# GpSimd and VectorE jump ahead within a block of instruction memory in a linear-attention kernel

## The chip, the cores and the metric

The kernel runs on one core of a Trainium2 chip. The metric is the device time of one execution in microseconds, as the median of several runs. The core has five engines that run side by side, each with an instruction stream of its own: TensorE (PE), VectorE (DVE), ScalarE (ACT), GpSimd (POOL) and SyncE (SP). They wait for each other on semaphores. Data moves between the chip's main memory (HBM) and on-chip memory (SBUF) on 16 DMA engines, which work through queues that SP, ACT and POOL fill.

## The reference

For each of 8 x 12 heads, Q, K and V are 512 x 64 in 32-bit floats, and a ReLU takes the place of the softmax:

```
Q_feat, K_feat = max(0, Q), max(0, K)
KV    = K_feat^T V            (64 x 64 per head)
K_sum = sum of K_feat over the 512 rows
out   = (Q_feat KV) / (Q_feat . K_sum + 1e-10)
```

There is little arithmetic for the bytes: 37.75 MB are read and 12.58 MB written.

## The kernel before, in words

The 96 heads are worked in 12 tiles of 8 heads. A tile of Q, of K or of V is 128 partitions x 2048 elements, 1 MB in HBM. K and V of tile 0 are loaded as they are, by SP and ScalarE, inside a short part that the tile framework handles (lines 95 to 97). `tc.close()` and `tc.compile()` (lines 99 and 100) end that part: all engines meet there. Everything behind is written by hand, engine by engine, with semaphores.

GpSimd (`PL`) issues all other loads. Line 101 is its first instruction behind the closing: it loads Q of tile 0. It then builds an identity matrix (lines 124 to 126), and issues K, V and Q of tiles 1 to 11 in order (`load`, line 114), the DMA turning 32-bit floats into bf16 on the way. The buffers hold 6 tiles, so from tile 7 on a load waits until VectorE and ScalarE have used the tile that lies there. GpSimd also issues the stores of tiles 0 to 9 (`store`, line 122), SP those of tiles 10 and 11.

VectorE (`VE`) first clears two tiles (lines 289 and 290), casts the identity and makes masks from it (292 to 302). Then it waits for K and V of tile 0 and per tile makes masked, ReLU-ed K (`kf`, line 248) and masked V (`vo`, line 254), copies Q (line 260), computes the denominators and their reciprocals (279 to 287), and multiplies the result out of PSUM by them (line 273), which is what a store waits for.

TensorE runs a loop over the tiles (line 198): it transposes Q, forms K^T V, multiplies Q by it, and transposes back. Line 94, ahead of the tile part, already places TensorE's stream at the start of a block of 256 instructions in the same way that the change uses for two other engines. ScalarE copies out of PSUM and applies the ReLU to Q. Last, SP waits for the final stores and clears the semaphores (lines 323 to 328).

The instructions of an engine lie one behind the other in memory, 64 bytes each, and the engine's sequencer has them fetched by DMA in blocks. In the profile these fetches are the queues of the kind "instruction".

Of the kernel before, what the change touches and what calls it, by code (L numbers as in the profile page):

```python
# [5 lines left out]
def kernel(  # L6
# [25 lines left out]
    PE, PL, VE, AC, SP = nc.tensor, nc.gpsimd, nc.vector, nc.scalar, nc.sync  # L32
# [11 lines left out]
    def sems(*names):  # L44
        new = [nc.alloc_semaphore(n) for n in names]
        handles.extend(new)
        return new
# [40 lines left out]
    def land(name):  # L88
        landed[name], = sems(name)
        return landed[name]  # L90
# [7 lines left out]

    tc.close()
    tc.compile()  # L100
    PL.dma_start(out=q_all[:, RING], in_=Qr[0], single_packet=True).then_inc(land("q0"), 16)
    run_of = {0: 0}

# [253 lines left out]
```

## Time and profile before

| | us |
|---|---|
| median of 3 runs | 124.32 |
| fastest and slowest of them | 124.25, 124.49 |
| the profiled execution, its own time | 124.49 |
| its span, first to last instruction of the kernel | 122.7 |
| VectorE busy / TensorE busy / ScalarE busy | 87.7 / 86.2 / 79.4 |
| GpSimd busy | 27.6 |

The span leaves out what the runtime runs ahead of the kernel's first instruction and behind its last; the own time is 1.79 us longer. In the rows of the page, the line "DMA" gives in tenths how busy the 16 DMA engines are in 40 slices of the span, and the part on queues gives packets, megabytes and the share of the 16 engines' span. In a timeline a row reads: start, duration, engine, line, operation, output and input, and in brackets the idle time before it and what ended it. Beside the views, the trace keeps a record of each DMA packet (queue, start, duration, size) and of each instruction that is not counted as busy (branches, waits); some numbers below come from these records. Times in them are from the start of the span.

### The profile page before, as it was taken

The page shows a single profiled execution, that of the slowest core. Times are in us where ns is not written, and L with a number is a line of the kernel's source. Part 1 is how long each engine was busy: PE and PEld are TensorE (multiplying, and loading weights), DVE is VectorE, ACT ScalarE, POOL GpSimd, SP SyncE. Part 2 cuts the span into 40 slices and gives each one's busy share as a digit, 9 for nine tenths or more (in the row PEclk, how much of TensorE's full clock was granted, in tenths as well). Part 3 has the DMA queues.
Part 4 walks back from the last instruction along what each step waited for, and adds up shares of the span by engine and source line. Part 5 has one row for each costly group of instructions (what it writes and reads, how often), then busy time and mean ns, then how long its engine had stood idle before and what let it go on. Part 6 is the DMA issues. An engine that isn't in the chain of part 4 may idle for free.

```text
span 122.7 us, 3406 instructions
## 1 busy us (share of the span) xinstructions
PE 86.2 (70%) x1480; PEld 73.4 (60%) x1480; DVE 87.7 (71%) x163; ACT 79.4 (65%) x109; POOL 27.6 (23%) x50
## 2 busy tenths in 40 slices
PE   0000099998998989899898998989898199491000
PEld 0000099986896958779595887958687189271000
DVE  1808806499999899999989999899992983761000
ACT  0043062999988888998888989888998196600000
POOL 1899900042140603409201001010010010000000
PEclk9999999999999999999999999999999999999555
DMA  2999999999999999999999999999999999999994
GB/s 64 414 319 214 214 214 214 214 211 214 214 214 211 215 212 215 212 214 214 214 212 214 214 214 214 214 214 350 239 204 286 430 430 427 419 430 430 427 427 190
DMA packets 6915, 32.54 MB, mean 265 GB/s; under 512 B 768, under 2 KB 768, under 8 KB 5120
## 3 DMA queue, kind: packets, MB, share of 16 engines
q0 software_dynamic: 6336, 28.31, 92.9%
q1 hardware_dynamic: 432, 3.15, 6.2%
q10 hardware_dynamic: 144, 1.05, 2.2%
q8 instruction: 1, 0.02, 0.1%
q14 instruction: 2, 0.02, 0.0%
HBM read 37.75 MB, written 12.58 MB: 410 GB/s over the span
## 4 chain that ended last, share of the span: by engine, by line
DMA 39%; PE 28%; DVE 20%; issue 1%; POOL 1%; ACT 1%; DVEq 0%; SPq 0%
DMA q_all<-in_Q_dram 32%; DVE o_sb L273 13%; PE ps_kv L173 12%; DMA o_sb<-in_K_dram 7%; PE ps_o L154 7%; PE ps_q L166 6%; PE ps_o L194 4%; DVE kf L248 3%; DVE vo L254 2%; DVE q_sb L260 1%; ACT ot L234 1%; POOL v_all L114 1%; POOL k_all L114 0%; DVE den L284 0%; PE ps_q L186 0%
## 5 line engine op out<-in xcount | busy, mean ns | idle before, releaser
L273 DVE TENSOR_TENSOR o_sb<-ps_o,rec 128x1024 f32<-128x1024 f32 x24 | 28.3, 1219 | 6.0 <-PE ps_o L154 6.0
L234 ACT COPY ot<-ps_o 128x1024 f32<-128x1024 f32 x24 | 24.2, 1013 | 7.6 <-PE ps_o L194 6.2
L173 PE MATMUL ps_kv<-vo,kf 64*128 64x132 bf16 x768 | 27.9, 227 | 0.0
L220 ACT ACTIVATE qt_sb<-ps_q 128x1024 bf16<-128x1024 bf16 x24 | 23.4, 1030 | 5.7 <-PE ps_q L166 5.7
L154 PE MATMUL ps_o<-ident,ot 128*128 128x128 f32 x208 | 25.7, 277 | 1.1 <-ACT ot L234 1.1
L173 PEld LDWEIGHTS ps_kv<-vo,kf 64*128 64x128 bf16 x768 | 24.2, 98 | 2.9 <-DVE vo L254 0.2
L154 PEld LDWEIGHTS ps_o<-ident,ot 128*128 128x128 f32 x208 | 22.6, 142 | 2.8 <-ACT ot L234 1.4
L166 PE MATMUL ps_q<-ident,q_sb 128*128 128x128 bf16 x192 | 13.6, 227 | 15.1 <-DVE q_sb L260 15.0
L248 DVE TENSOR_SCALAR kf<-k_all,mask_k 128x1024 bf16<-128x1024 bf16 x44 | 18.4, 461 | 5.3 <-PE ps_kv L173 4.0
L194 PE MATMUL ps_o<-qt_sb,kvd 128*128 128x256 bf16 x104 | 15.7, 275 | 9.1 <-DVE o_sb L273 8.6
L166 PEld LDWEIGHTS ps_q<-ident,q_sb 128*128 128x128 bf16 x192 | 11.6, 101 | 17.6 <-DVE q_sb L260 15.0
L225 ACT CAST kvd<-ps_kv 64x260 bf16<-64x260 f32 x48 | 18.0, 375 | 6.2 <-PE ps_kv L173 5.8
L194 PEld LDWEIGHTS ps_o<-qt_sb,kvd 128*128 128x128 bf16 x104 | 8.2, 98 | 14.3 <-DVE o_sb L273 12.5
L254 DVE TENSOR_SCALAR vo<-v_all,mask_v 128x1024 bf16<-128x1024 bf16 x33 | 14.9, 481 | 0.5 <-DMA v_all<-in_V_dram 0.5
L122 POOL DMA_DIRECT2D out_dram<-o_sb x10 | 5.3, 533 | 37.1 <-DVE o_sb L273 37.1
L114 POOL DMA_DIRECT2D k_all<-in_K_dram x11 | 6.6, 596 | 31.3 <-DVE vo L254 31.1
L214 ACT ACTIVATE vo<-v_all,mask_v 128x1024 bf16<-128x1024 bf16 x11 | 12.7, 1155 | 0.3
L260 DVE COPY q_sb<-q_all 128x2048 bf16<-128x2048 bf16 x12 | 8.3, 689 | 2.0 <-DMA q_all<-in_Q_dram 2.0
L114 POOL DMA_DIRECT2D v_all<-in_V_dram x11 | 8.4, 768 | 0.0
L186 PE MATMUL ps_q<-kvd,qt_sb 128*128 128x16 bf16 x208 | 7.5, 180 | 0.0
L186 PEld LDWEIGHTS ps_q<-kvd,qt_sb 128*128 128x128 bf16 x208 | 7.3, 96 | 0.2
L279 DVE SCALAR_TENSOR_TENSOR own<-ps_q,mask_h 128x256 f32<-128x256 f32 x12 | 5.0, 415 | 2.4 <-PE ps_q L186 2.4
(21 smaller groups left out, 28.7 us busy)
## 6 DMA issues: line engine op xcount, KB each, us to landing
out_dram<-o_sb POOLq DMA_DIRECT2D x10, 1024.0 KB, 39.1
q_all<-in_Q_dram POOLq DMA_DIRECT2D x12, 512.0 KB, 35.2
k_all<-in_K_dram POOLq DMA_DIRECT2D x11, 512.0 KB, 31.8
v_all<-in_V_dram POOLq DMA_DIRECT2D x11, 512.0 KB, 33.7
out_dram<-o_sb SPq DMA_DIRECT2D x2, 1024.0 KB, 8.8
o_sb<-in_V_dram ACTq DMA_DIRECT2D x1, 1024.0 KB, 8.4
o_sb<-in_K_dram SPq DMA_DIRECT2D x1, 1024.0 KB, 8.6
```

The lines of the kernel that those rows point to most:

```text
L114: PL.dma_start(out=t[:, to:to + n], in_=X[o:o + n].rearrange("n p f -> p n f"), single_packet=True).then_inc(land(f"{c}{o}"), 16)
L154: t = PE.transpose(ps_o[j][:, P * v:P * v + P], ot[:, 8 * j + v].rearrange("p h c -> p (h c)"), ident32)
L166: t = PE.transpose(dst[:, u], q_sb[:, j * (U // 2) + u], ident)
L173: t = PE.matmul(ps_kv[:, half, 0:2 * (D + 2)].rearrange("p (t d) -> p t d", t=2), kf[g][rows, r].rearrange("p s d -> p (s d)"), vo[g][rows ...
L186: t = PE.matmul(ps_den[:, u], qt_sb[:, u], kvd[:, :, 0:2 * D1:2 * D1 - 1], start=True, stop=True, skip_group_check=True)
L194: t = PE.matmul(ps[:, h], kvd[:, 4 * j + h, 1:2 * D + 1], q[:, :, 4 * j + h, :], start=True, stop=True, skip_group_check=True)
L220: AC.activation(qt_sb[:, j * (U // 2):(j + 1) * (U // 2)], ps_q[j].bitcast(bf16).rearrange("p (u f) -> p u f", u=U // 2), Act.Relu)
L225: t = AC.copy(kvd[64 * c:64 * c + 64, s::2, c * D1:c * D1 + D1].rearrange("p (g t) d -> p g t d", t=2), ps_kv[64 * s:64 * s + 64, :, 0:2 * ...
L234: t = AC.copy(ot[:, :, 4 * j:4 * j + 4], ps_o[j].rearrange("p (h u c) -> p u h c", h=4, u=U))
L248: VE.tensor_scalar(kf[g][:, :, s, :], k_rows(o, g), scalar1=0.0, scalar2=mask_k[:, s:s + 1], op0=Alu.max, op1=Alu.mult)
L254: x = VE.tensor_scalar(vo[g][:, :, t, 2:D + 2], v_rows(o, g), scalar1=mask_v[:, t:t + 1], scalar2=None, op0=Alu.mult)
L273: VE.tensor_tensor(dst[:, rs], ps_o[j].rearrange("p (r d) -> p r d", d=D), rec[o % 2][:, rs].unsqueeze(2).to_broadcast([P, R, D]), op=Alu. ...
```

## The change

Directly behind the closing of the tile part, and ahead of line 101, each of GpSimd and VectorE gets one directive on where its next instruction is to lie. It says: the next instruction goes to the slot that is 112 (for VectorE 120) slots past a multiple of 128 slots, a slot being one instruction of 64 bytes. The slots that are left out are filled with padding when the program is loaded. With `max_nops=0` the engine runs none of the padding: the first of these slots is a branch to the wanted place. No instruction is added beside the branch, none is removed, and the order on every engine stays as it was. Behind the change GpSimd has 16 slots left in its block of 128, and VectorE 8.

```diff
     tc.close()
     tc.compile()
+
+    PL.addr_align(128, offset=112, max_nops=0)
+    VE.addr_align(128, offset=120, max_nops=0)
     PL.dma_start(out=q_all[:, RING], in_=Qr[0], single_packet=True).then_inc(land("q0"), 16)
     run_of = {0: 0}
```

## The prediction

> **What bounds the kernel now.** I read the page's transfer rows first, then the end of the chain of waits, the start of GpSimd's and VectorE's timelines, and last the DMA view in short windows, because what the change moves is instruction memory, and its refills are DMA traffic.
>
> ```profile
> span 122.7 us, 3406 instructions
> ...
> DMA  2999999999999999999999999999999999999994
> ...
> q0 software_dynamic: 6336, 28.31, 92.9%
> ...
> q8 instruction: 1, 0.02, 0.1%
> q14 instruction: 2, 0.02, 0.0%
> HBM read 37.75 MB, written 12.58 MB: 410 GB/s over the span
> ...
> DMA 39%; PE 28%; DVE 20%; issue 1%; POOL 1%; ACT 1%; DVEq 0%; SPq 0%
> ```
>
> The DMA row is 9 in 38 of 40 slices, from 3 us to 120 us: the 16 DMA engines are the bound, not the chain's 39%. The chain runs through TensorE and VectorE because loads wait for buffers to come free, but behind those waits the DMA queue is never empty. The stage view gives it in numbers: DMA share 1.01 to 1.07 in every stage from 3 to 120 us, 427 GB/s from 98 to 120 us. VectorE's last work of weight, the last normalisation, ends at 110.80 us and SP's wait for the last store takes 11.4 us; so compute has some 9 us to spare at the end.
>
> ```profile
> 2.58 0.49 DVE L289 MEMSET kvd<- 128x520 f32 x1 [2.58 <-PEq L100]
> 2.93 0.67 POOL L101 DMA_DIRECT2D q_all<-in_Q_dram  x1 [2.48 <-POOLq L100]
> 3.45 1.76 DVE L290 MEMSET ot<- 128x2048 f32 x1 [0.38 <-issue]
> ...
> 9.65 1.42 DVE L248 TENSOR_SCALAR kf<-o_sb,mask_k 128x1024 bf16<-128x1024 f32 x2 [3.23 <-DMA o_sb<-in_K_dram]
> 9.72 0.81 POOL L114 DMA_DIRECT2D v_all<-in_V_dram  x1
> ```
>
> The timeline of the start, in which the jumps fall. VectorE is idle for 3.23 us ahead of its first real work at 9.65 us. GpSimd issues loads far ahead of what the DMA engines can move: 0.52 us apart, for 1 MB read that takes them 2.46 us.
>
> The DMA view of three windows (42.5 to 43, 48 to 48.5, 123 to 126 us) gives this one line in each:
>
> ```profile
> q14 instruction: 1, 0.01, 4.0%
> ...
> q14 instruction: 1, 0.01, 4.0%
> ...
> q14 instruction: 1, 0.01, 0.7%
> ```
>
> Each is a refill of instruction memory. The packet records put them at 42.55, 48.14 and 124.04 us, each 8,192 bytes and 0.32 us on one DMA engine; 8,192 bytes are 128 instructions of 64 bytes, the block the change counts in. TensorE's, on queue 8, is 16,384 bytes at 1.87 us.
>
> **The change, part by part.**
>
> *The two jumps.* Each engine gets one branch over padding. TensorE's like jump (line 94) has a record of 0.31 us, its loop branches 0.08 to 0.23 us; the floor is nothing, the padding itself being skipped. I take 0.31 us each, the same kind of jump. *VectorE:* its seven set-up instructions move from 2.58 to about 2.9 us and end at 6.75 instead of 6.43; the idle 3.23 us cover that, so 0. ScalarE's table load (6.51 us) waits for the same set-up, but its first activation waits for the V load at 9.29: 0. *GpSimd:* line 101 moves from 2.93 to 3.24 us and all 33 loads behind it on its queue by as much; the identity that VectorE waits for is 0.3 us later, again under the 3.23 us. Would the DMA engines run dry? The first packet of GpSimd's queue is at 6.70 us. Until then K0 and V0, 2.10 MB, fill all 16 engines: 0.17 MB moved by 3 us, then 415 GB/s, so they alone last to 3.0 + 1.93/0.415 = 7.65 us. GpSimd has 0.95 us, the jump takes 0.31: 0 on the path. SP and ScalarE issue K0 and V0 ahead of the change.
>
> *Where blocks are crossed.* From line 101 GpSimd has 49 records, VectorE from line 289 has 177. GpSimd now starts at slot 112: 16 records on (the Q load, the identity's five, ten loads) it crosses at the V load of 9.72 us. It ends at slot 161. VectorE starts at slot 120: seven set-up instructions and the wait for K0, then it crosses at the kf of 9.65 us; the second crossing is 128 records later, the kf at 82.33 us; it ends at slot 297. Which engines cross at 42.55 and 48.14 before, the trace doesn't name. TensorE's jump ends at 1.13 and its refill starts at 1.87, so 0.74 us earlier is 41.8 and 47.4 us; VectorE's copy at 41.72 and GpSimd's load at 41.91 both fit the first. Neither crossing made its engine wait: VectorE's iterations stay 7.26 us apart through both.
>
> *What a refill costs.* The completion writes of each load on the 16 engines are a clock with a period of 2.457 us. At 42.55 one engine falls back by 0.52 us (44.69 expected, 45.21 seen), at 48.14 another by 0.31, and they keep it. So a refill costs 0.31 to 0.52 us on one engine, and the end moves only if that engine is the last, or is made the last. The last store completes on the 16 engines from 120.58 to 121.77, and on one at 122.04 us. After the change there may be up to two more refills in the loaded window (VectorE's second, GpSimd's), so +0 to +0.52 us if the two hit different engines and +1.04 us if both hit the last one; below, a refill gone from the last engine gives at most 122.04 - 121.77 = 0.27 us. With 12 engines finishing at 121.45 or earlier, at least 0.59 us behind, I take 0.
>
> On this the Trainium skill, "Runtime: NRT & Kernel Launch", section "Instruction fetch mechanics", says that crossing a block is one bump of a DMA queue and mostly hidden, with blocks of 16 KiB. The trace agrees for the engine that crosses, not on the size (8,192 bytes but for TensorE), and the 0.31 to 0.52 us on a DMA engine are real. By that rule the term is 0 whatever engine is hit; by the row it is 0 to 1.04 us.
>
> *Sum.* The profiled execution took 124.49 us: span 122.70 and 1.79 around it. 0 + 0 + 0 added to it; it is 0.17 us above the median of 124.32. I forecast 124.35 for the median.
>
> **The rivals.**
>
> *A, the refill of the closing goes (faster).* The fetch at 124.04 ends at 124.37, 0.12 us ahead of the run's own 124.49. If an engine stands there waiting for it, and this engine is GpSimd or VectorE, the jumps take that boundary away: they end at slots 161 and 297, with 95 and 87 slots left in their blocks. The gain is between the transfer's 0.32 us and 0.74 + 0.32 = 1.06 us from crossing to landing: 124.0 down to 123.26, and 123.7 between them. For: the fetch is the last DMA record of all, and so near the end. Against: both refills in the middle made nobody wait, and it may be another engine's.
>
> *B, a further refill hits the last DMA engine (slower).* VectorE crosses twice inside the kernel now, GpSimd once. If one of these refills lands on the engine that ends at 122.04, or at 0.31 to 0.52 us on one of the three that end at 121.70 to 121.77, the last store is later by up to 0.52 us: 124.4 to 124.84; 125.36 with two. It decides as soon as an engine is delayed past 122.04. For: the 0.52 us seen. Against: four of 16 engines are near enough, and the block behind the engine's last may not be fetched at all.
>
> *C, GpSimd's jump lands on a block not at hand (slower).* Jump plus fetch, 0.31 + 1.06 = 1.37 us, against 0.95 us of cover: an idle stretch of 0.42 us, 124.74. Against: TensorE's jump went on to its next record at 1.19 us, before its fetch had begun.
>
> *D, the refill leaves the last engine (faster).* It would have to move to before 3 us, where the engines still stand idle (DMA share 0.22 up to 3 us); then -0.27: 124.05. Against: by my count the crossings are at 9.7 us.
>
> **How the numbers follow.** 0.2% is 0.25 us, about what a measurement of this kernel can tell from no change (its three runs span 124.25 to 124.49). Chances: my forecast 0.44; A 0.25; B 0.20; C 0.06; D 0.05. Faster 0.30 (A and D), same 0.44, slower 0.26. The likeliest case's own range is 124.1 to 124.57. The range for 8 in 10 reaches down into A to 123.6 and up over B and C to 124.9; left out are the far halves of A and a double hit.
>
> **What would show it.** Right: line 101 between 2.95 and 3.3 us, GpSimd's first packet before 7.65 us, no window with a DMA share under 1 from 3 to 120 us; an instruction refill near 10 us instead of 42 us; VectorE's kf at 9.65 within 0.3 us. A shows as no q14 packet behind the span and a smaller rest around it (1.79 us now) with an unchanged span. B shows as two or more extra q14 packets and a last completion past 122.1 us. C shows as DMA slices under 9 near 7 us. I am wrong altogether if the span moves by more than 0.5 us.

## The result, and the profile after

The changed kernel takes 123.88 us (median of 20 runs, 123.58 to 124.34) against 124.37 us for the kernel before in the same comparison (20 runs): a ratio of 0.996, 95% interval 0.9948 to 0.9972. That is 0.49 us faster. I had forecast no change (124.35 us); the measured time is nearly that of rival A (123.7 us).

Where the time went is told by two numbers of each run: its span and the rest around it (its own time less its span). The span did not get shorter: median 122.50 us after, 122.40 us in the 29 runs of before that were measured next to the first experiments. The rest fell from 1.80 us (1.74 to 1.84) to 1.31 us (1.26 to 1.63; all but one run under 1.37). The whole gain is in the rest. (The median time of those 29 runs is 124.21 us; against them the gain in time is 0.33 us, since the span after is some 0.1 us longer.)

The page of the kernel after, its first lines, transfers and queues:

```profile
span 122.6 us, 3408 instructions
...
DMA  2999999999999999999999999999999999999994
...
q14 instruction: 4, 0.03, 0.1%
```

Two instructions more than before: the two branches. Queue 14 moved four blocks inside the span instead of two, and the DMA row is as full as it was. The DMA view of after, in windows of 12 to 14.5, 48.4 to 49 and 79.5 to 80.5 us:

```profile
q14 instruction: 2, 0.02, 1.6%
...
q14 instruction: 1, 0.01, 3.4%
...
q14 instruction: 1, 0.01, 2.0%
```

By the packet records these are at 12.37, 13.85, 48.64 and 79.81 us. The window from 122 to 126 us, which held a packet before (124.04 us), holds none now. The start, in the timeline of after (start, duration, operation, idle time before it):

```profile
2.78 0.49 DVE L292 MEMSET kvd<- 128x520 f32 x1 [2.78 <-PEq L100]
3.08 0.67 POOL L104 DMA_DIRECT2D q_all<-in_Q_dram  x1 [2.63 <-POOLq L100]
...
9.88 0.62 POOL L117 DMA_DIRECT2D v_all<-in_V_dram  x1
```

Each jump costs its engine 0.15 to 0.20 us (2.58 to 2.78, 2.93 to 3.08), and nothing of it reaches the end. One thing at the start is new. It stands in the chain of waits, between the landing of K0 and VectorE's first `kf`; of before, then of after:

```profile
9.55 0.03 issue
9.58 0.02 DVEq L147
9.60 0.05 issue
9.65 1.42 DVE kf L248 x2
```

```profile
10.16 0.03 issue
10.19 0.02 DVEq L150
10.21 0.45 issue
10.65 1.43 DVE kf L251 x2
```

After VectorE's wait for K0 is over, the kernel before starts 0.05 us later, the kernel after 0.45 us. (That K0 landed 0.6 us later in this execution is another matter: it landed at 9.58 us with VectorE's jump alone, and at 9.93 in a run with no jump at the start.) This `kf` is the instruction that I had counted to slot 128, the first of the next block. So this crossing has a price of its own, 0.40 us, and it was paid though the refill was not awaited: the next packets of queue 14 come at 12.37 us.

Other crossings show no such pause. VectorE crosses at the `kf` of 40.51 us in the kernel before (its place is found below), and a second time at the `kf` of 82.82 us in the kernel after:

```profile
39.48 0.88 DVE L254 TENSOR_SCALAR vo<-v_all,mask_v 128x1024 bf16<-128x1024 bf16 x2
40.51 0.90 DVE L248 TENSOR_SCALAR kf<-k_all,mask_k 128x1024 bf16<-128x1024 bf16 x2
```

```profile
82.55 0.35 DVE L290 RECIPROCAL rec<-den 128x32 f32<-128x32 f32 x1
82.82 0.78 DVE L251 TENSOR_SCALAR kf<-k_all,mask_k 128x1024 bf16<-128x1024 bf16 x2
```

The first is held by TensorE in every iteration, and starts 0.14 to 0.17 us after the `vo` ahead of it in all from 33 us on; here it is 0.15. The second starts before the reciprocal ends. Nor do GpSimd's loads around its own crossing at 9.88 us come further apart than 0.52 us. So the 0.40 us are seen only where the engine, done waiting, has nothing else in hand; that waits or queued work hide them elsewhere is argued, not shown.

The closing is what the runtime runs behind the kernel's last instruction on each engine. Once the last store has landed (121.92 us in the kernel after), no data moves that could cover such a pause: it could be what the rest lost. That is the theory that the experiments test.

### The profile page after: what moved, and what is told of

Its sections match the earlier page's. It is cut to its first block, busy times and chain, and to the rows that moved or that the text cites. A ratio compares the mean times of both kernels' runs of the same rounds, so it can differ in the third digit from the quotient of the medians.

```text
span 122.6 us, 3408 instructions
## 1 busy us (share of the span) xinstructions
PE 87.0 (71%) x1480; PEld 74.4 (61%) x1480; DVE 87.7 (72%) x163; ACT 79.3 (65%) x109; POOL 27.9 (23%) x50
## 4 chain that ended last, share of the span: by engine, by line
DMA 39%; PE 29%; DVE 20%; issue 2%; POOL 1%; ACT 1%; DVEq 0%; SPq 0%
DMA q_all<-in_Q_dram 31%; DVE o_sb L276 13%; PE ps_kv L176 12%; DMA o_sb<-in_K_dram 8%; PE ps_o L157 7%; PE ps_q L169 6%; PE ps_o L197 4%; DVE kf L251 3%; DVE vo L257 2%; DVE q_sb L263 1%; ACT ot L237 1%; POOL v_all L117 1%; POOL k_all L117 0%; DVE den L287 0%; PE ps_q L189 0%
## 5 line engine op out<-in xcount | busy, mean ns | idle before, releaser
L176 PE MATMUL ps_kv<-vo,kf 64*128 64x132 bf16 x768 | 28.5, 230 | 0.0
L176 PEld LDWEIGHTS ps_kv<-vo,kf 64*128 64x128 bf16 x768 | 24.9, 100 | 2.8 <-issue 0.4
L117 POOL DMA_DIRECT2D k_all<-in_K_dram x11 | 7.8, 706 | 31.2 <-DVE vo L257 31.1
L117 POOL DMA_DIRECT2D q_all<-in_Q_dram x11 | 9.1, 824 | 0.0
L117 POOL DMA_DIRECT2D v_all<-in_V_dram x11 | 8.9, 812 | 0.0
```

Source lines behind the costliest of these rows:

```text
L117: PL.dma_start(out=t[:, to:to + n], in_=X[o:o + n].rearrange("n p f -> p n f"), single_packet=True).then_inc(land(f"{c}{o}"), 16)
L176: t = PE.matmul(ps_kv[:, half, 0:2 * (D + 2)].rearrange("p (t d) -> p t d", t=2), kf[g][rows, r].rearrange("p s d -> p (s d)"), vo[g][rows ...
```

## The experiments

"Room" is the number of slots from the start of an engine's closing to the end of the block. All runs compute the full result. In the table, medians of n runs; the rest is good to some 0.05 us, since spans are given in tenths.

| run | GpSimd's room | VectorE's room | n | own time | span | rest |
|---|---|---|---|---|---|---|
| before | not set | 8 (see below) | 29 | 124.21 | 122.40 | 1.80 |
| after | 95 | 87 | 20 | 123.88 | 122.50 | 1.31 |
| e1_pool_only | 95 | 8 | 12 | 124.03 | 122.40 | 1.65 |
| e2_dve_only | not set | 87 | 12 | 124.03 | 122.40 | 1.55 |
| e4_dve_end8 | 95 | 8, no branch | 12 | 124.08 | 122.40 | 1.66 |
| e3_pool_end8 | 8 | 87 | 5 | 127.40 | 125.70 | 1.68 |
| e6_two_ends | 128 | 128 | 12 | 123.95 | 122.60 | 1.32 |
| e7_dve_room64 | 128 | 64 | 10 | 123.85 | 122.55 | 1.30 |
| e8_dve_room24 | 128 | 24 | 6 | 123.87 | 122.55 | 1.31 |
| e9_dve_room8 | 128 | 8, no branch | 10 | 124.03 | 122.40 | 1.65 |
| e10_dve_room2 | 128 | 2 | 7 | 123.90 | 122.60 | 1.31 |
| e11_pool_room8 | 8 | 128 | 10 | 124.18 | 122.45 | 1.72 |
| e12_pool_room24 | 24 | 128 | 5 | 123.72 | 122.40 | 1.32 |
| e5_all_ends | 128 | 128 | 11 | 124.42 | 123.10 | 1.32 |

### Which of the two jumps it is

```diff
+    PL.addr_align(128, offset=112, max_nops=0)
```

> GpSimd's directive alone. Theory P (the refill of the closing at 124.04 us is GpSimd's, and the 0.50 us that the rest around the span lost hangs on it): 0.4 to 0.6 us faster than before, the rest 1.3 us, no instruction packet behind the span. Theory V (it is VectorE's): no change, rest 1.8 us, the packet still there. Theory S (the gain is in the span, by which DMA engine the refills hit): rest 1.8 us, and the span 0.1 to 0.3 us shorter.

```diff
+    VE.addr_align(128, offset=120, max_nops=0)
```

> VectorE's directive alone. Theory P: no change against before, rest 1.8 us, the late packet still there, and a refill of VectorE near 80 us. Theory V: 0.4 to 0.6 us faster, rest 1.3 us, no late packet. Theory S: rest 1.8 us, span 0.1 to 0.3 us shorter.

Neither theory that gives it to one engine holds. GpSimd's jump alone takes 0.15 us off the rest, VectorE's alone 0.25, both 0.49; the spans are the same, so theory S is out too. By time: GpSimd's alone 0.998 (0.9962 to 0.9998), VectorE's alone 0.9987 (0.9971 to 1.0003), which is not clear of no change. With VectorE's alone the rest also varies more than elsewhere, from 1.41 to 1.66 us.

The late packet is GpSimd's. In the run with VectorE's jump alone the DMA view of 122 to 126 us still has it, at 123.59 us by its record; in the run with GpSimd's alone the same window has no such line:

```profile
q14 instruction: 1, 0.01, 0.7%
```

But VectorE's jump, which leaves this packet in place, gains more than GpSimd's, which takes it away. So the packet can't be the whole price; it is a sign that GpSimd crossed there.

The pause at the crossing shows again with VectorE's jump alone, in the chain of that run:

```profile
9.61 0.02 DVEq L149
9.63 0.45 issue
10.08 1.53 DVE kf L250 x2
```

### Putting the boundary back into the closing

```diff
+    PL.addr_align(128, offset=112, max_nops=0)
+    VE.addr_align(128, offset=71, max_nops=0)
```

> Both directives, but VectorE's offset is 71 in place of 120: its last multiplication lies at slot 247, 8 slots ahead of a block's end, so that it crosses in the closing. Theory V: back to the time before, rest 1.8 us, a packet behind the span. Theory P: as the changed kernel, rest 1.3 us; unless any engine's crossing in the closing costs, then 1.8 us here and in the run before alike.

The rest is 1.66 us, between the two theories, and the same as with GpSimd's directive alone. The trace says why: there is no branch on VectorE in it, so its stream lay at slot 71 all along. With 177 records from there it ends at slot 247, and its room in the kernel before is 8 slots. The pause at the first `kf` is gone as well:

```profile
9.60 0.02 DVEq L150
9.62 0.05 issue
9.68 1.48 DVE kf L251 x2
```

This run and the one with GpSimd's directive alone are thus the same kernel in effect, and in both the refill near 42 us is back (41.52 and 41.61 us). So that refill of the kernel before was VectorE's. The other, near 48 us, is there in every run (47 to 51 us), and so is neither engine's.

```diff
+    PL.addr_align(128, offset=71, max_nops=0)
+    VE.addr_align(128, offset=120, max_nops=0)
```

> Both directives, but GpSimd's offset is 71 in place of 112: its last store lies at slot 119, 8 slots ahead of a block's end, so that it crosses in the closing. Theory P: back to the time before (rest 1.8 us) and a packet behind the span; if it is dearer to cross there than where it did before, more. Theory V: as the changed kernel, rest 1.3 us.

3.2 us slower than before (1.0244, 1.0216 to 1.0271), all of it in the span, which is 3.3 us longer. The chain of this run begins with it:

```profile
2.40 5.57 issue
7.97 0.67 POOL q_all L104
```

After the branch GpSimd stood for 5.57 us (0.68 us with the offset 112). Slot 71 of its own block must have lain behind it already, so the jump went into the next block, and that had to be brought in: the packet records have a refill at 6.25 us. Line 104 issues at 7.97 us instead of 3.08, GpSimd's first packet comes at 9.35 us instead of 6.86, and K0 and V0 don't last that long. The stage view of the run (stage, length, busy time of PE, PEld, DVE, ACT, POOL, clock, DMA share, GB/s):

```profile
3.00:6.00 3.00, 0.00 (x0) 0.00 (x0) 2.04 (x2) 0.00 (x0) 0.00 (x0) 1.00 0.99 404
6.00:9.00 3.00, 0.00 (x0) 0.00 (x0) 0.00 (x0) 0.00 (x0) 0.89 (x2) 1.00 0.59 246
9.00:12.00 3.00, 0.00 (x0) 0.00 (x0) 2.52 (x7) 1.07 (x1) 2.74 (x6) 1.00 0.85 143
```

The DMA engines are idle for 0.41 x 3.0 + 0.15 x 3.0 = 1.7 us from 6 to 12 us, and time that a full DMA queue loses doesn't come back. (The rest of the 3.2 us I have not traced.) The Trainium skill, "Runtime: NRT & Kernel Launch", section "Instruction fetch mechanics", says that a taken branch to a block that isn't among the two that an engine holds has to wait for a fetch. The trace agrees in the effect, with 5.57 us.

The rest of this run, 1.68 us, is between the two theories as well: with 8 slots of room GpSimd's closing costs 0.37 us against the changed kernel's 1.31, and no packet of queue 14 lies behind the span. And if slot 71 lay behind GpSimd, it ended at slot 121 or later in the kernel before, with 7 slots of room or fewer.

### The same gain without a jump at the start

To part the closing from all that happens at the start, the directives go to the ends of the streams, into the stretch in which the engine has nothing left to do:

```diff
     for i in range(done, NO - 2):
         store(PL, i)
+    PL.addr_align(128, offset=0, max_nops=0)
...
     norm(NO - 1)
+    VE.addr_align(128, offset=0, max_nops=0)
```

> No directive at the start; instead one behind GpSimd's last store and one behind VectorE's last multiplication, each to the start of the next block of 128 (offset 0), in the stretch in which both engines have nothing left to do. Theory C (a block boundary inside an engine's closing costs 0.15 to 0.25 us of the rest, on each of the two): rest 1.3 us as in the changed kernel, span as before, 0.4 to 0.5 us faster than before. Theory R (the gain comes from the early refills, or from where the start of the streams lies): rest 1.8 us, no change.

The rest is 1.32 us: the full gain in the rest, with no change at the start and with VectorE's refill left at 41.84 us. Theory R is out. Both directives made a branch (GpSimd's at 98.12 us, VectorE's at 109.97). The span is 0.2 us longer than in the comparison's 31 runs of before (122.60 against 122.40), so the time is 123.95 against 124.23 us, 0.9984 (0.9973 to 0.9995). The two jumps add refills at 101.74 and 113.59 us; whether these make the 0.2 us was not tested by itself.

Then VectorE's offset is changed, with GpSimd's left at 0:

```diff
     norm(NO - 1)
+    VE.addr_align(128, offset=64, max_nops=0)    # 104, 120, 126 in the other three
```

> As with two ends, but VectorE's closing starts at slot 64 of its new block, so with 64 slots of room. Theory C: rest 1.3 us if its closing is shorter than 64 instructions, 1.55 us or so if it is longer. Theory A (not the crossing, but being at slot 0 to 48 of a block): 1.65 us.

> As with two ends, but VectorE's closing starts at slot 104, with 24 slots of room (before it was 8). Theory C: if the closing has more than 24 instructions it crosses, rest 1.65 us as with GpSimd's directive alone; if fewer, 1.3 us. Theory A: 1.65 us.

> As with two ends, but VectorE's closing starts 8 slots ahead of a block's end, the room that it had before (it ended at slot 247 without a jump). Theory C (crossing in the closing costs): rest 1.55 to 1.65 us, as with GpSimd's directive alone, 0.25 to 0.35 more than with 24 slots of room. Theory J (the jump into another block or the refill at idle time is what helps, wherever in the block it lands): rest 1.3 us.

> The same with 2 slots of room. Theory C with the crossing falling in the first wait of the closing, where VectorE stands idle: rest 1.3 us. Theory C without such a wait in the first two instructions, or with a price wherever the boundary lies: rest 1.55 to 1.65 us. Theory J: 1.3 us; this run tells them apart only together with the one of 8 slots.

With 128, 64 and 24 slots of room the rest is 1.32, 1.30 and 1.31 us; with 8 slots it is 1.65; with 2 slots 1.31 again. Theory A is out: the offsets 64 and 104 do as well as 0.

Theory J is not tested by the run with 8 slots. It has one instruction less than the runs with 64, 24 and 2 slots; the first lines of the pages with 24 and with 8:

```profile
span 122.5 us, 3408 instructions
```

```profile
span 122.4 us, 3407 instructions
```

The one that it lacks is VectorE's branch. The next slot of its stream is 248, which is 120 past 128 already, so the directive did nothing, and VectorE ran as in the kernel before. (This confirms the count of 177 from slot 71.) No run has both a jump on VectorE and 8 slots of room. What speaks against theory J is the changed kernel beside the run with GpSimd's directive alone: they differ by VectorE's jump at the start, within its own block, and the rest falls from 1.65 to 1.31 us with nothing added at the end. With theory R out as well, what is left is the place of VectorE's closing: with 8 slots of room it costs 0.34 us, and by this theory the closing has at most 24 instructions.

The run with 2 slots fits. Its jump, by 6 slots, stays in the block, and the refill that follows the crossing is at 117.32 us, inside the span: VectorE's last multiplication ends at 112.77 us, and SP waits for the stores until 122.32. So by this refill VectorE crossed while it still had to wait for the others.

```diff
     for i in range(done, NO - 2):
         store(PL, i)
+    PL.addr_align(128, offset=120, max_nops=0)    # 104 in the other
...
     norm(NO - 1)
+    VE.addr_align(128, offset=0, max_nops=0)
```

> VectorE with the whole block ahead of it (offset 0), GpSimd's closing 8 slots ahead of a block's end. Theory C: rest 1.45 to 1.6 us, as with VectorE's directive alone (1.55), and an instruction packet behind the span if that packet was GpSimd's. Theory J: rest 1.3 us.

> The same with 24 slots of room for GpSimd. Theory C: 1.3 us if its closing is as short as VectorE's, under 24 slots; 1.45 to 1.6 us if it is longer. Theory J: 1.3 us.

GpSimd behaves alike: 1.72 us with 8 slots of room, 1.32 with 24. Both runs have GpSimd's branch (98.11 and 98.14 us) and differ by 16 slots in its target alone, so for GpSimd theory J is out, and the place of the boundary is shown to be the cause of its 0.40 us. That is more than the 0.24 us that the rest of the run with VectorE's jump alone lies over 1.31; GpSimd's room there was, by the run with its offset of 71, 7 slots or fewer, and how many isn't known. No packet of queue 14 lies behind the span in either run, nor in the one with 8 slots for VectorE: the price is paid with no refill on record. The run with 24 slots for GpSimd, 123.72 us and 0.996 (0.9945 to 0.9974), is the changed kernel's equal, not better by the intervals.

### All five engines

```diff
+    PE.addr_align(256, offset=0, max_nops=0)     # behind TensorE's loop
+    AC.addr_align(128, offset=0, max_nops=0)     # ahead of ScalarE's last wait
+    SP.addr_align(128, offset=0, max_nops=0)     # ahead of SP's last wait
```

(on top of the two ends)

> The same with all five engines: ScalarE and SP jump to a new block of 128 ahead of their last waits, TensorE to a new block of 256 behind its loop. Theory C, if no other engine crosses in its closing: rest 1.3 us as with two. If SP (22 records) or TensorE cross there too: 0.15 to 0.25 us less for each, rest 0.9 to 1.15 us. If a jump that is waited for stands on the path (SP's directly ahead of its wait for the stores): the span 1 us or more longer.

The rest stays at 1.32 us, so the other three engines cross nothing there that counts. But the span is 0.70 us longer, and the kernel slower than before: 1.0016 (1.0005 to 1.0026). The queues of this run:

```profile
span 123.1 us, 3411 instructions
...
q8 instruction: 2, 0.03, 0.1%
q14 instruction: 6, 0.05, 0.1%
```

Four refills of 8,192 bytes lie from 102.00 to 116.00 us, and TensorE's 16,384 bytes at 116.04 us take 0.96 us of a DMA engine that has some 6 us of stores left. The last store completes at 120.63 to 121.95 us on 15 engines and at 122.40 on one. That it is these late refills which hold the last engine back is argued from the times; which packet delayed which engine was not isolated.

## Why the prediction was wrong

**The bound** held. The DMA share is 0.99 to 1.07 in every stage from 3 to 120 us after the change too, and the run with GpSimd's offset of 71 showed what an idle DMA queue costs.

**The two jumps** were right as a zero, and over-priced: 0.15 and 0.20 us instead of 0.31. GpSimd's line 104 came at 3.08 us, inside the stretch I gave, and its first packet at 6.86 us, well ahead of 7.65. VectorE's first `kf` came 1.00 us later and not within 0.3: 0.6 us were K0's landing, which I have not explained, and 0.40 the pause.

**Where blocks are crossed** was counted right for VectorE's first crossing, as the pause shows. The refill that belongs to the second comes at 79.81 us, 3.0 us ahead of the counted `kf` (82.82 us after), and not behind it as the first ones; why is open. The count itself is borne out by the run with 8 slots of room for VectorE, in which the branch at slot 248 fell away. The early refills came 2 to 4 us later than I expected. My guess at what the kernel before crossed was half of it: VectorE at 42.55 us. The crossing itself was at 40.51 us, 2.04 us ahead of its refill, so the 0.74 us that I took from TensorE's jump did not hold for it. I did not count where the closings of the two engines lay, since the trace doesn't give the streams' places; the run with VectorE's offset of 71 did, by leaving the branch out.

**The step that failed** is the one from "Neither crossing made its engine wait" to the sum: I took a crossing to cost no more than its refill's share of a DMA engine, wherever it lies, and carried the rest of 1.79 us over unchanged. The sentence is right for the crossing at 40.51 us, where VectorE had to wait for TensorE in any case; it says nothing of a crossing that no wait covers. One at the start cost 0.40 us, and in the closing a boundary with 8 slots of room costs 0.34 us (VectorE) and 0.40 us (GpSimd) of the rest. So the term that the sum held at nothing, the change of the rest, was -0.49 us (1.80 to 1.31).

**What a refill costs**, 0 to 1.04 us, was the term I worked at most, and it came to nothing that the span can show: two more refills in the loaded window, and 122.50 against 122.40 us. In the profiled run the last completion is at 121.92 us, against 122.04 before.

**Rival A** named the right place and the right sign, with the marks that came true (no packet behind the span, a smaller rest, the span the same). Its mechanism was wrong: not an engine waiting for the refill at 124.04 us, since the engine without that packet gained more, and the boundary costs as much where no refill is seen. Its sign that the packet ends 0.12 us ahead of the run's own 124.49 us was no sign: how much of the rest lies ahead of the span, no record shows. Against 1.31 us, VectorE's boundary costs 0.34 us alone, GpSimd's, where it lay in the kernel before, 0.24 alone, and both 0.49 together, less than the sum. That fits engines that wait for one another in the closing and pay partly at the same time, which is argued, not shown: no trace shows the closing's instructions.

**Rival B**'s further refills came, and did not hit. **Rival C** didn't happen at the offset of 112, but its mechanism is real at 71, and I had it too cheap: 5.57 us and 3.2 us of time, not 1.37 and 0.42. **Rival D** isn't seen.

## What to carry to other kernels

In a kernel that is bound by DMA from end to end, a few tenths can still lie outside the span: look at the own time less the span as a number of its own, since it is far steadier from run to run (1.74 to 1.84 us in the kernel before) than the time. Where no wait and no queued work covers it, crossing into the next block of instruction memory cost some 0.4 us here, so put the crossing where the engine waits anyhow; at the end of a stream, leave room in the block for the closing. Here 24 slots were enough and 8 were not. And never jump into a block that isn't there yet on the engine that feeds the DMA queues.

## What the runs showed of the hardware that was not expected

- Crossing a block boundary right behind a wait cost VectorE 0.40 us, though the next refill came only 2 us later (0.45 us from the end of the wait to the first `kf` instead of 0.05). Crossings under a wait or under work (40.51, 82.82 us) show no pause.
- In the closing the price depends on the place within a few slots: with 2 slots of room for VectorE none, with 8 slots 0.34 us, with 24 none; for GpSimd 0.40 us with 8 slots, none with 24.
- A jump into the next block cost GpSimd 5.57 us at the start of the kernel, of which 3.9 us passed before the refill's packet even began (branch at 2.37, packet at 6.25 us).
- A refill among full DMA queues sets one DMA engine back: in the kernel before one engine fell back by 0.52 us at 42.55 us and another by 0.31 us at 48.14, and both kept that for over 30 us.
